# The DRAM round trips of the transposed attention units, issued from GpSimd's queue

## The chip, the cores and the metric

One core of one Trainium2 chip runs the whole layer. The metric is the device time of the kernel in microseconds; runs are compared by their median.

## What is computed

One decoder layer over 512 tokens of width 2048, all in fp32. The input is normalised, one wide projection feeds three head groups, and their gated outputs go through one output projection, with a residual add and a final normalisation:

```python
h = rmsnorm(x, norm_g)
proj = h @ w_in
...
o_cmp, o_slc = nsa_compressed_and_selected(q_a, k_cmp, v_cmp, ...)
o_win = banded_attention(q_a, ..., slopes_a, NSA_WINDOW, None)
o_a = gate[..., 0:1] * o_cmp + gate[..., 1:2] * o_slc + gate[..., 2:3] * o_win
y_a = o_a.reshape(bsz, T, A_WIDTH) * jax.nn.silu(a_z)
...
h_b = mlstm_chunkwise(...)
y_b = h_b.reshape(bsz, T, B_WIDTH) * jax.nn.silu(b_z)
...
o_c = banded_attention(..., alibi_slopes(C_HEADS), SWA_WINDOW, sinks)
y_c = o_c.reshape(bsz, T, C_WIDTH) * jax.nn.silu(c_z)
mix = jnp.concatenate([y_a, y_b, y_c], axis=-1)
return x + mix @ w_out
```

Groups A and C have 8 heads of 64, group B has 4 heads of 256.

## The kernel before

TensorE works through the columns of both projections in a fixed order: sixteen groups of input columns (`groups`) and four of output columns (`outs`). Every weight is split into a high and a low part (`wh`, `wl`), and every product is three matmuls (line 1149). A group is cut into pieces of 256 rows of the weight (512 for `ck`). The loop at the end of the program takes one piece at a time: it splits the piece two ahead (ScalarE makes `wh` in lines 162 and 164, VectorE makes `wl` in lines 170 and 172), issues the matmuls of the present one, and then starts the load of the piece five ahead (`dma_piece`, line 140). There are three buffers `raw` for these loads, so a load waits until VectorE has read the piece three before it.

Everything else runs beside this loop in "lanes", Python generators that advance by one `yield` after each set of matmuls (`step`). Their instructions fall between those of the projections, and each engine and each queue takes its instructions strictly in the order in which the program wrote them. Nothing is reordered at run time.

From the group `bo0` on, the softmax lanes run: `a_scores` and `a_out` for group A, `c_scores` and `c_out` for group C, which starts at `bz0`. One step of `a_out` takes two heads and one of two branches (selected blocks or window): eight such steps, called A0 to A7 here. Group C has four, C0 to C3, two heads each. The probabilities come out with queries on partitions, and the product with V wants keys there. The transposition goes through DRAM: `flip` takes the step's tiles one after the other (six in an A step, four in a C step). For each, `flip_out` has VectorE transpose it in 32x32 blocks into `sq` (line 613) and writes `sq` to a DRAM tile `far` (line 615); two tiles later, `flip_in` reads `far` back with the blocks in their new places (line 621, tiles `ptT` for A and `cptT` for C). The read waits for the landing of its write. After the last read and a pause of a few yields the matmuls of the step are placed in TensorE's order: line 952 (`oT`) for A, line 1035 (`coT`) for C. TensorE waits at that place if the last tile has not landed. Group B's hidden states take the same way, with four writes per pair in `hb_post` and the four reads in `ev_bz` (`hbT`), long after.

SP issues all weight loads, all writes and reads of the flips, and at the end the output. In this stretch GpSimd's queue (POOL) holds only five loads: `fg`, the final norm's gain (line 1168), and `xr` four times, the residual input (line 1174). They wait until the input projection has done with the tiles whose room they take.

Of the kernel before, what the change touches and what calls it, by code (L numbers as in the profile page):

```python
# [27 lines left out]
T, D, P = 512, 2048, 128  # L28
# [32 lines left out]
def hymba_layer(ctx, tc, x, norm_g, w_in, w_out, pe_k, w1_k, w2_k, pe_v, w1_v, w2_v, conv_w, conv_b,  # L61
                i_bias, f_bias, mnorm_g, sinks, final_g, consts, out):
    nc = tc.nc
    PE, ACT, DVE, POOL, SP = nc.tensor, nc.scalar, nc.vector, nc.gpsimd, nc.sync
# [9 lines left out]
    def U(name, dt=F32):  # L74
        return ar.tile([P, 516], dt, tag="u", name=name)
# [3 lines left out]
    def WK(name):  # L79
        return ps.tile([P, 512], F32, tag="wk", bufs=4, name=name)  # L80
# [223 lines left out]
    p = WK("gT")  # L304
# [303 lines left out]
    def flip_out(src, tag, bufs):  # L608


        n = src.shape[1]
        sq, far = U("sq"), dr.tile([P * 512], F32, name="far", tag=tag, bufs=bufs)
        DVE.transpose(sq[:, :n].rearrange("p (j b t) -> p b j t", j=4, t=32),  # L613
                      src.rearrange("p (b k j) -> p b j k", j=4, k=32))
        SP.dma_start(far[:P * n].rearrange("(p f) -> p f", p=P), sq[:, :n])
        return far, n

    def flip_in(far, name):

        dst, (src, n) = U(name), far  # L620
        SP.dma_start(dst[:, :n].rearrange("p (q f) -> p q f", q=4),
                     src[:P * n].rearrange("(q p f) -> p q f", q=4, p=P))
        return dst[:, :n].rearrange("p (q b t) -> p b q t", q=4, t=32)

    def hb_post(pair, ssq):
        yield from pause(3)
        for t in range(4):
            hb, th = B["hb", pair, t], U("bsq")
            for q in range(2):
                ACT.activation(th[:, q * 256:(q + 1) * 256], hb[:, q * 256:(q + 1) * 256], AF.Square,  # L630
                               accum_out=ssq[:, 2 * t + q:2 * t + q + 1])
            yield
        r = S("br", 8, 2)
        rsqrt(r, ssq, 256, "b")
        DVE.tensor_scalar(r, r, 0.5, None, op0=OP.mult)
        yield
        for t in range(4):
            hb = B["hb", pair, t]
            for q in range(2):
                s = slice(q * 256, (q + 1) * 256)  # L640
                DVE.tensor_scalar(hb[:, s], hb[:, s], r[:, 2 * t + q:2 * t + q + 1], None, op0=OP.mult)
            yield

        B["hbT", pair] = []
        for t in range(4):
            B["hbT", pair].append(flip_out(B.pop(("hb", pair, t))[:, :512], "hbT", 8))
            yield
# [3 lines left out]
    def ev_bz(pair):  # L651
        def ev(c, acc):
            z = U("zf")
            scaled(z[:, :512], acc)
            if c == 0:
                B["hbT", pair] = [flip_in(x, "hbT") for x in B["hbT", pair]]
            start(bz_post(pair, c, z))
        return ev
# [204 lines left out]
    def flip(parts, name):  # L863

        far, back = [], []
        for i in range(len(parts)):
            far.append(flip_out(parts[i], "far", 8))
            parts[i] = None
            if i >= 2:
                back.append(flip_in(far[i - 2], name))  # L870
            yield
        return back + [flip_in(x, name) for x in far[-2:]]
# [284 lines left out]
    for pos, (g, i) in enumerate(pieces):  # L1157
        np_ = KT // g.kps
        nct = g.n // P if g.mode == "F" else NT
        if i == 0:  # L1160
# [10 lines left out]
            if g.mode == "O":  # L1171
                n = int(g.name[3])
# [65 lines left out]
```

## Time and profile before

| | |
|---|---|
| median of 3 runs | 1028.22 us (1027.75 to 1030.64) |
| the profiled execution: its time | 1031.22 us |
| its span, first to last instruction | 1029.5 us |
| TensorE (PE) busy | 98% |
| VectorE (DVE), ScalarE (ACT) busy | 57%, 46% |
| GpSimd (POOL) busy | 2% |
| granted TensorE clock, mean | 0.989 of full speed |

All stretches are in us from the start of the span. A row of the timeline has start, duration, engine, line, operation, output and inputs, how many instructions are merged, and in brackets the idle time of the engine before the first of them and what ended it. A row of DMA issues has output and input, queue, operation, count, size of each and the median time from issue to landing. "PEclk" is the granted TensorE clock as a share of full speed: 1.00 is 2.4 GHz, 0.50 is 1.2 GHz.

### The profile page before, as it was taken

How to read it: one execution, taken by the hardware profiler on the slowest of the kernel's cores; microseconds unless marked ns; L12 is line 12 of the kernel's file. 1: busy time of each engine (PE TensorE's matmuls, PEld its weight loads, DVE VectorE, ACT ScalarE, POOL GpSimd, SP SyncE). 2: the span in 40 equal slices, each digit the busy share in tenths (PEclk: the TensorE clock that was granted, in tenths of full speed). 3: DMA queues.
4: the chain of work that ended last, by engine and by line, in shares of the span. 5: the costliest groups of instructions: out<-in, count | busy, mean ns of one | idle time of the engine just before them, and what ended most of it. 6: DMA issues, size and time to landing. Idle time of an engine off the chain costs nothing.

```text
span 1029.5 us, 13708 instructions
## 1 busy us (share of the span) xinstructions
PE 1007.5 (98%) x4967; PEld 835.0 (81%) x4967; DVE 585.6 (57%) x1253; ACT 477.5 (46%) x991; POOL 21.5 (2%) x40
## 2 busy tenths in 40 slices
PE   9999999999999999999999999999899899999996
PEld 7988888888888888888888788878777788888885
DVE  4563266664284847435566577856676575424434
ACT  6753244443253536234467474755654542323324
POOL 2400000000000000000000000000000000000000
PEclk9999999999999999999999999999999899999998
DMA  8633323232313244232335556555564685433214
GB/s 238 173 109 100 103 65 103 62 103 82 103 61 103 62 127 100 82 111 74 103 105 175 175 172 193 148 160 163 164 200 133 241 276 173 127 100 100 85 61 164
DMA packets 121092, 133.22 MB, mean 129 GB/s; under 512 B 23557, under 2 KB 81261, under 8 KB 120897
## 3 DMA queue, kind: packets, MB, share of 16 engines
q1 hardware_dynamic: 117792, 125.66, 40.9%
q0 software_dynamic: 2240, 6.23, 1.8%
q8 instruction: 39, 0.64, 0.3%
q10 hardware_dynamic: 992, 0.46, 0.2%
q14 instruction: 29, 0.23, 0.1%
HBM read 111.88 MB, written 20.45 MB: 129 GB/s over the span
## 4 chain that ended last, share of the span: by engine, by line
PE 86%; DVE 6%; DMA 5%; issue 1%; ACT 1%; SPq 0%; ACTq 0%; DVEq 0%
PE acc L1149 72%; DMA far<-sq 3%; DVE sq L613 2%; PE oT L952 2%; PE sp L561 1%; DMA ptT<-far 1%; PE acc L316 1%; PE acc L315 1%; PE acc L314 1%; DVE wl L172 1%; PE coT L1035 1%; PE sc L902 1%; PE sc L901 1%; PE xT L285 1%; DVE pp L905 0%
## 5 line engine op out<-in xcount | busy, mean ns | idle before, releaser
L1149 PE MATMUL acc<-hTh,wh 128*128 128x512 f32 x720 | 283.6, 394 | 0.0
L1149 PE MATMUL acc<-hTh,wl 128*128 128x512 f32 x720 | 281.5, 391 | 0.0
L1149 PE MATMUL acc<-hTl,wh 128*128 128x512 f32 x720 | 281.2, 391 | 0.0
L172 DVE SCALAR_TENSOR_TENSOR wl<-raw,gcol,wh 128x512 fp32r<-128x512 f32 (+1 forms) x256 | 179.0, 718 | 125.1 <-ACT wh L164 124.7
L164 ACT ACTIVATE wh<-raw,gcol 128x512 fp32r<-128x512 f32 (+1 forms) x256 | 171.2, 695 | 150.9 <-PE acc L1149 124.2
L1149 PEld LDWEIGHTS acc<-hTh,wl 128*128 128x128 f32 x720 | 135.4, 188 | 28.8
L1149 PEld LDWEIGHTS acc<-hTh,wh 128*128 128x128 f32 x720 | 135.6, 188 | 27.7 <-issue 1.7
L1149 PEld LDWEIGHTS acc<-hTl,wh 128*128 128x128 f32 x720 | 135.7, 188 | 25.8
L1149 PE MATMUL acc<-wh,hTh 128*128 128x512 f32 x256 | 101.2, 395 | 0.0
L1149 PE MATMUL acc<-wh,hTl 128*128 128x512 f32 x256 | 100.1, 391 | 0.0
L1149 PE MATMUL acc<-wl,hTh 128*128 128x512 f32 x256 | 99.9, 390 | 0.0
L1149 PE MATMUL acc<-wh,mixh 128*128 128x512 f32 x224 | 88.6, 396 | 0.0
L1149 PE MATMUL acc<-wh,mixl 128*128 128x512 f32 x224 | 88.1, 393 | 0.0
L1149 PE MATMUL acc<-wl,mixh 128*128 128x512 f32 x224 | 88.0, 393 | 0.0
L170 DVE TENSOR_TENSOR wl<-raw,wh 128x512 fp32r<-128x512 f32 x56 | 38.4, 689 | 55.7 <-ACT wh L162 55.4
L162 ACT CAST wh<-raw 128x512 fp32r<-128x512 f32 x56 | 34.0, 617 | 76.3 <-PE acc L1149 64.0
L1149 PEld LDWEIGHTS acc<-wh,hTl 128*128 128x128 f32 x256 | 48.0, 188 | 10.5
L1149 PEld LDWEIGHTS acc<-wh,hTh 128*128 128x128 f32 x256 | 48.1, 188 | 9.4 <-issue 0.4
L1149 PEld LDWEIGHTS acc<-wl,hTh 128*128 128x128 f32 x256 | 48.1, 188 | 9.0
L907 ACT ACTIVATE pp<-pp,nmx 128x512 f32<-128x512 f32 (+3 forms) x64 | 35.8, 559 | 35.1 <-DVE nmx L905 35.0
L905 DVE CUSTOM_DVE_ANT_0 pp<-sc,dmast 128x512 f32<-128x512 f32 (+3 forms) x64 | 31.1, 485 | 35.2 <-PE sc L902 35.0
L1149 PEld LDWEIGHTS acc<-wh,mixl 128*128 128x128 f32 x224 | 42.1, 188 | 10.0
(285 smaller groups left out, 1255.0 us busy)
## 6 DMA issues: line engine op xcount, KB each, us to landing
raw<-in_w_in_dram SPq DMA_DIRECT2D x80, 512.0 KB, 3.8
raw<-in_w_in_dram SPq DMA_DIRECT2D x68, 256.0 KB, 2.9
raw<-in_w_out_dram SPq DMA_DIRECT2D x32, 512.0 KB, 3.9
far<-sq SPq DMA_DIRECT2D x48, 256.0 KB, 2.8
ptT<-far SPq DMA_DIRECT2D x32, 256.0 KB, 3.9
xr<-in_x_dram POOLq DMA_DIRECT2D x4, 1024.0 KB, 8.3
x<-in_x_dram SPq DMA_DIRECT2D x12, 256.0 KB, 5.3
raw<-in_w_in_dram SPq DMA_DIRECT2D x8, 384.0 KB, 3.2
```

The source lines that it names most:

```text
L162: ACT.copy(t["h"][:, q], raw[:, j + q])
L164: ACT.activation(t["h"][:, q], raw[:, j + q], AF.Copy, scale=gcol[:, k:k + 1])
L170: DVE.tensor_tensor(t["l"][:, q], raw[:, j + q], f(t["h"][:, q]), op=OP.subtract)
L172: DVE.scalar_tensor_tensor(t["l"][:, q], raw[:, j + q], gcol[:, k:k + 1], f(t["h"][:, q]), op0=OP.mult, op1=OP.subtract)
L285: PE.transpose(p[:, q * P:(q + 1) * P], X[t][c][:, q * P:(q + 1) * P], ident)
L314: PE.matmul(acc[:, :416], HH(k, *s), G0H[k][:, :416], start=(k == 0), stop=False)
L315: PE.matmul(acc[:, :416], HL(k, *s), G0H[k][:, :416], start=False, stop=False)
L613: DVE.transpose(sq[:, :n].rearrange("p (j b t) -> p b j t", j=4, t=32), src.rearrange("p (b k j) -> p b j k", j=4, k=32))
L905: DVE.tensor_tensor_reduce(b, sp[:, :nk], dmast[:, 512 - nk:], scale=-(2.0 ** -(h + 1)), scalar=3.0e38, op0=OP.add, op1=OP.min, accum_out= ...
L907: later(lambda b=b, h=h, j=j, st=st: ACT.activation(b, b, AF.Exp, scale=-1.0, bias=st[h][0][:, j:j + 1], accum_out=st[h][1][:, j:j + 1]))
L952: PE.matmul(ob[64 * q:64 * q + 64, j * P:(j + 1) * P], VG[i][:, vo + 64 * g:vo + 64 * g + 64], tt[h][j, i], start=False, stop=(br == 2 and ...
L1149: PE.matmul(accs[c][:, :n], a, b, start=(k == 0 and q == 0), stop=(k == KT - 1 and q == 2))
```

## The change

Two words. The write to `far` and the read from it, which SP issued, are issued by GpSimd:

```diff
         DVE.transpose(sq[:, :n].rearrange("p (j b t) -> p b j t", j=4, t=32),
                       src.rearrange("p (b k j) -> p b j k", j=4, k=32))
-        SP.dma_start(far[:P * n].rearrange("(p f) -> p f", p=P), sq[:, :n])
+        POOL.dma_start(far[:P * n].rearrange("(p f) -> p f", p=P), sq[:, :n])
         return far, n

     def flip_in(far, name):

         dst, (src, n) = U(name), far
-        SP.dma_start(dst[:, :n].rearrange("p (q f) -> p q f", q=4),
+        POOL.dma_start(dst[:, :n].rearrange("p (q f) -> p q f", q=4),
                      src[:P * n].rearrange("(q p f) -> p q f", q=4, p=P))
```

It covers 72 writes and 72 reads (48 `ptT`, 16 `cptT`, 8 `hbT`). The orders of PE, DVE and ACT are the same in both kernels.

SP's queue at step A1 before. `raw` is a weight load, `far<-sq` a write, `ptT<-far` a read:

```order
L140 DMA raw<-in_w_in_dram 128x2x512
L615 DMA far<-sq 128x512
L615 DMA far<-sq 128x256
L621 DMA ptT<-far 128x4x128
L615 DMA far<-sq 128x512
L621 DMA ptT<-far 128x4x128
L615 DMA far<-sq 128x512
L621 DMA ptT<-far 128x4x64
L140 DMA raw<-in_w_in_dram 128x2x512
L615 DMA far<-sq 128x256
L621 DMA ptT<-far 128x4x128 x2
```

SP's queue in the same part of the program now, from the loads of the compression weights (`w_3554`) to the first outputs:

```order
L756 DMA w_3554<-in_cmp_w_v_dram 128x8x64
L140 DMA raw<-in_w_in_dram 128x2x512 x36
L140 DMA raw<-in_w_in_dram 128x4x128 x4
L140 DMA raw<-in_w_in_dram 128x2x512 x24
L140 DMA raw<-in_w_out_dram 128x2x512 x32
L1099 DMA out_dram<-y 128x512 x3
```

The writes and reads have gone, and the weight loads follow one another. The writes and reads keep their order among themselves on POOL.

POOL's queue at the start of the output projection, what it held before and holds now. `fg` and the first `xr` stand ahead of step C3's flips:

```order
+L621 DMA hbT<-far 128x4x128 x4
 L1168 DMA fg<-in_final_norm_g_dram 128x2048
-L1174 DMA xr<-in_x_dram 128x4x512 x4
+L1174 DMA xr<-in_x_dram 128x4x512
+L615 DMA far<-sq 128x384
+L615 DMA far<-sq 128x512
+L615 DMA far<-sq 128x384
+L621 DMA cptT<-far 128x4x96
+L615 DMA far<-sq 128x512
+L621 DMA cptT<-far 128x4x128
```

Before, `fg` was the first DMA on POOL after the parameters of the beginning. Now the flips of A0 to A7 and of C0 to C2 and both sets of `hbT` reads stand ahead of it, and three of the four `xr` come after C3's flips.

## Rows read from the trace of the kernel before

**Rows 1.** Busy time, share of the span and instructions of each engine (page, part 1)

```profile
PE 1007.5 (98%) x4967; PEld 835.0 (81%) x4967; DVE 585.6 (57%) x1253; ACT 477.5 (46%) x991; POOL 21.5 (2%) x40
```

**Rows 2.** PE's waits over the span: us in total, times, longest us

```profile
PE oT L952 <- DMA ptT<-far: 8.7, 5, 3.8
PE coT L1035 <- DMA cptT<-far: 2.7, 2, 1.6
```

**Rows 3.** Timeline of PE where it waited, at steps A1, A4, A6, A7, C1

```profile
579.55 0.44 PE L952 MATMUL oT<-ptT,vg 128*64 128x128 f32 x4 [1.68 <-DMA ptT<-far]
...
677.25 2.65 PE L952 MATMUL oT<-ptT,vg 128*64 128x128 f32 x38 [0.36 <-DMA ptT<-far]
...
740.41 0.98 PE L952 MATMUL oT<-ptT,vg 128*64 128x128 f32 x8 [2.59 <-DMA ptT<-far]
...
774.07 1.34 PE L952 MATMUL oT<-ptT,vg 128*64 128x128 f32 x16 [3.82 <-DMA ptT<-far]
...
807.92 0.40 PE L1035 MATMUL coT<-cptT,vg 128*64 128x128 f32 x2 [1.13 <-DMA cptT<-far]
809.90 1.33 PE L1035 MATMUL coT<-cptT,vg 128*64 128x128 f32 x10 [1.58 <-DMA cptT<-far]
```

**Rows 4.** Timeline of PE at steps A0, A2, A5 and C3, without a wait

```profile
548.67 2.75 PE L952 MATMUL oT<-ptT,vg 128*64 128x128 f32 x40
...
612.82 2.35 PE L952 MATMUL oT<-ptT,vg 128*64 128x128 f32 x40
...
705.91 2.40 PE L952 MATMUL oT<-ptT,vg 128*64 128x128 f32 x40
...
865.38 1.75 PE L1035 MATMUL coT<-cptT,vg 128*64 128x128 f32 x28
```

**Rows 5.** Last reads of A2, A5, C3: DMA issues at 607.5, 703.1, 860.8

```profile
ptT<-far SPq DMA_DIRECT2D x1, 128.0 KB, 2.9
...
ptT<-far SPq DMA_DIRECT2D x1, 128.0 KB, 2.2
...
cptT<-far SPq DMA_DIRECT2D x1, 256.0 KB, 2.9
```

**Rows 6.** Busy time by stretch: stretch, us, each engine (count), PEclk, DMA, GB/s

```profile
580.40:583.80 3.40, 3.40 (x34) 3.36 (x31) 0.00 (x0) 0.00 (x0) 0.00 (x0) 0.50 0.76 279
...
809.10:815.90 6.80, 6.00 (x32) 4.87 (x33) 0.00 (x0) 1.33 (x2) 0.00 (x0) 0.50 0.81 272
```

**Rows 7.** Chain that ended last: start, us, what; two sets of 34 matmuls

```profile
580.21 3.85 PE oT L952 x34
...
677.72 2.18 PE oT L952 x34
```

**Rows 8.** Writes and reads of the flips on SP: duration min/median/max, ns

```profile
L615 SPq DMA_DIRECT2D far<-sq x72: 319/333/1021, 532.3 to 855.6; - x72
L621 SPq DMA_DIRECT2D ptT<-far x48: 359/376/1082, 536.8 to 770.9; - x48
```

**Rows 9.** Timeline of POOL, the loads of the last 250 us

```profile
795.98 0.56 POOL L1168 DMA_DIRECT2D fg<-in_final_norm_g_dram  x1 [756.82 <-PE acc L1149]
...
838.59 1.49 POOL L1174 DMA_DIRECT2D xr<-in_x_dram  x2 [41.28 <-PE acc L1149]
```

**Rows 10.** DMA issues from 23.1 to 23.6, one after the other

```profile
raw<-in_w_in_dram SPq DMA_DIRECT2D x1, 152.0 KB, 2.9
raw<-in_w_in_dram SPq DMA_DIRECT2D x1, 128.0 KB, 2.1
raw<-in_w_in_dram POOLq DMA_DIRECT2D x1, 8.0 KB, 3.2
```

**Rows 11.** Landing of all 72 writes, us (line 615)

```profile
DMA to landing us min/median/max: 1.7/2.7/7.2
```

**Rows 12.** DMA issues from 797.8 to 802: a write of step C1

```profile
far<-sq SPq DMA_DIRECT2D x1, 192.0 KB, 7.2
```

**Rows 13.** Readers of `xr`: duration, first and last start us

```profile
L1075 DVE TENSOR_TENSOR y<-acc,xr x16: 682/690/692, 882.6 to 1020.2; 128x512 f32<-128x512 f32 x16
```

## The prediction

> **What bounds the kernel now.** I read the engine shares first: TensorE (PE) is busy 98% of the span [rows 1], so only what leaves PE idle, or slows its clock, can move the time. Next PE's waits: after the start it waits for nothing but the last reads of the flips, 8.7 us at A steps and 2.7 us at C steps, 11.4 in all [rows 2]. It never waits for a weight, so sparing the weight loads their wait behind the flips is worth nothing by itself. The timeline says which steps: A1 (1.7), A4 (0.4), A6 (2.6), A7 (3.8) and C1 (1.1 and 1.6) [rows 3]. The rest of the 8.7 is a second pause of 0.2 in A1.
>
> Of the steps without a wait, A0 has no slack: its 40 matmuls take 2.75 us where A2's take 2.35 [rows 4], so the last tile lands while they run. A2's last read is issued at 607.5 and lands 2.9 later, at 610.4 [rows 5]; PE uses it at 612.8, a slack of 2.4. Two more are as roomy (A3 3.0, C2 2.5, the same pair of rows). A5 lands at 705.3 and is used at 705.9, slack 0.6; C3 lands at 863.7 and is used at 865.4, slack 1.7 [rows 4, 5].
>
> A stall has a second price. After the stalls of A1, A6, A7 and C1 the granted clock stands at 0.50 (1.2 GHz): 3.4 us after A1, 6.8 after C1 [rows 6], and 3.4 after each of the other two. What 3.4 us of it cost is read from two sets of 34 equal matmuls, 3.85 us there and 2.18 at full clock [rows 7]: 1.7 us. So the flips now cost 11.4 us of idle time and about 8.5 (1.7 x 3 + 3.4) of slow clock, 20 in all. The change acts on these 20 us and on the steps that have no slack.
>
> **The change part by part.**
>
> *SP loses 144 issues.* Weight loads stand alone on SP and start when their buffer is free. PE does not wait for them, so I count nothing. Nor does the weight loads' waiting much delay the flips today: a load waits for VectorE to finish a split that stands ahead of the next transpose in VectorE's own order, so a write behind it loses only the load's issue, about 0.4 us.
>
> *POOL gains 144 issues.* On SP a write takes 0.33 us to issue and a read 0.38 [rows 8]. On POOL `fg`, with one row per partition like a write, takes 0.56, and two `xr`, with four rows per partition like a read, take 1.49, 0.75 each [rows 9]. At the end of a step one write and one read may stand ahead of the last write, 0.6 us longer than on SP; a weight load that often stood there has gone, 0.4 to 0.6. I count these against each other.
>
> *Each landing gets later.* The trace has no write or read of `far` on POOL. The nearest rows are three loads issued within half a microsecond: on SP 128 KB lands after 2.1 us and 152 KB after 2.9, on POOL 8 KB after 3.2 although it has the least to move [rows 10]. POOL's price is so between 0.3 and 1.1 us per DMA, less whatever the separate queue gives back. I take 0.6, near the middle. A step's tail is a last write, its landing, a last read, its landing: two landings, **1.2 us per step**, 0.6 and 2.2 at the ends. The Trainium skill, page "DMA: Bandwidth & Descriptors", section "Latency and other measured facts", gives about 0.6 us to the first byte for SP's path and about 1 us for GpSimd's; by it the estimate would be 0.8 per step and the estimate of the sum 2.4 us smaller, 3.3. The trace's pair reaches from less to nearly three times its 0.4 per landing.
>
> Where it falls: A0, A1, A4 and A6 have no slack, 4.8. A5 pays beyond its slack, 0.6. A2, A3, C2 and C3 are covered by their slack of 1.7 to 3. A7 shares its stretch with C0: ten writes and ten reads in one queue need 10 x 0.56 + 10 x 0.75 = 13.1 us of issue on POOL against 7.1 on SP [rows 8, 9], so I take 2.0 there. Together 7.4 us.
>
> *`fg` and the first `xr` move behind other flips.* Today they go out at 796.0 [rows 9], 2 MB in the middle of C1's flips, and a write of C1 needs 7.2 us to land [rows 12] against a median of 2.7 [rows 11]. In the new order they stand behind C2's flips and the second `hbT` reads, some 40 us later. The first reader of `xr` is at 882.6 [rows 13], so they still land in time. C1 is relieved by at most its 2.7 us of idle time and 3.4 of slow clock, 6.1. It also pays the 1.2 and has its own weight loads beside it, so I take half: 1.7 idle and 1.7 clock, **3.4 us gained**.
>
> *Clock.* With 1.2 us more A0 and A4 wait about 1.6 us each, about the smallest wait after which the trace shows 0.50 (1.7, A1); 0.4 at A4 had none after it [rows 3, 6]. I count one new stretch at the low level, 1.7.
>
> *Sum:* 7.4 - 3.4 + 1.7 = **5.7 us slower**. The profiled execution took 1031.2 (span 1029.5) and would take 1036.9 (1035.2); it lies 3.0 above the median of the runs, 1028.2, so the median becomes 1033.9.
>
> *Ends.* With 1.1 per landing, a step pays 2.2: A0, A1, A4, A6 8.8, A5 1.6, C3 0.5, A7 4, C1 gains nothing, three new stretches of slow clock 5.1: 20 slower, 1048. With 0.3 a step pays 0.6: 2.4 at the four, 0 at A5, 1 at A7, no new slow stretch, and C1 is relieved in full: 3.4 - 6.1, 2.7 faster, 1025.5.
>
> **The rivals.**
>
> *Faster: the flips' data no longer stands behind weight data.* On SP a write that follows a weight load lands after it: the median landing is 2.7 us, the shortest 1.7 [rows 11]. If the separate queue gives back this 1.0 at each of the two landings and POOL's price is at its lower end (0.3), a tail is 1.4 us shorter. A1 gains 1.4, A4 0.4, A6 1.4, A7 1.4, C1 2.7, 7.3 in all, and with the clock after C1 (3.4) nearly 11: 1017 to 1021, say 1019. It decides from the point where a landing on POOL beside weights is no later than one on SP behind them. For it: most landings today are well above the shortest. Against it: flips share the same DMA engines with weights whichever queue issues them, and weight loads which today wait behind a flip would now run beside it.
>
> *Nothing measurable:* the price per step is about 0.8, at the four 3.2, A5 0.2, A7 1.6, together 5.0, and C1's relief of 5 cancels it: 1028. The Trainium skill's page "DMA: Bandwidth & Descriptors", section "Issuing engines are not separate DMA queues", speaks for it: the engine that issues changes only the time of issue. The landings in rows 10 don't show equality.
>
> *Much slower: VectorE holds up GpSimd's issues.* If a POOL DMA must wait until a running VectorE instruction ends, each of the tail's two landings can lose up to a mean VectorE instruction, 585.6 us over 1253, 0.47 us [rows 1]: 0.9 per step, over A0, A1, A4 to A7 and C1 6.3 more, plus two slow stretches, 3.4: 1044. Against it: POOL's issues at 796 and 838 are no longer than 0.56 and 0.75 each [rows 9], with VectorE 57% busy over the span [rows 1]. The Trainium skill's page "SBUF — State Buffer", section "SBUF: two separate sides", states such a lock for some two-port VectorE instructions; no run here shows it.
>
> **How the numbers follow.** Forecast (2 to 16 slower) 0.50, much slower 0.06, nothing measurable 0.20, faster 0.24. About 0.3%, 3.1 us, is what a measurement of this kernel can tell from no change: faster means below 1025.1, slower above 1031.3. The forecast's lower edge lies inside "same", the rival "same" spreads a little to both sides; I give faster 0.25, same 0.20, slower 0.55. The likeliest case's own range is 1030 to 1044. The range over all cases, with half of "faster" in it, is 1019 to 1044.
>
> **What would show it.** Right: in the new profile A0, A1, A4, A5, A6 and A7 each wait 1 to 2 us more for `ptT`; writes and reads on POOL land 0.3 to 1.1 us later than on SP in comparable stretches; C1's wait shrinks and `fg` goes out after 830. Wrong: PE's waits for flips fall in sum below 11.4, or the medians of landing fall although POOL issues them (rival one); VectorE or ScalarE gets later by itself; or POOL's issues grow far beyond 0.75 us (rival three). A wait of PE for weights or for `xr` would be outside all of this.

## The result, and the profile after

The change costs 1.6%: 1044.41 us median (1042.63 to 1048.67) against 1027.99 for the kernel before on the same chip, a ratio of 1.016 with a 95% interval of 1.0123 to 1.0197. Slower was forecast, but by 5.7 us and not by 16.4, and the time lies just outside the range that ended at 1044.

The profiled execution took 1048.67 us, its span is 1046.9. That is 17.4 us more than the span of before, and the rows below say where they are. First the busy times and PE's waits, which answer to [rows 1, 2] (a row of waits: us in total, times, longest us):

```profile
PE 1009.7 (96%) x4967; PEld 836.2 (80%) x4967; DVE 585.9 (56%) x1253; ACT 477.1 (46%) x991; POOL 114.7 (11%) x184
...
PE oT L952 <- DMA ptT<-far: 25.5, 8, 8.3
PE coT L1035 <- DMA cptT<-far: 0.9, 2, 0.6
```

PE waits 16.8 us more at A steps and 1.8 less at C steps, and it is busy 2.2 us longer with the same 4967 instructions, which is the slower clock: together 17.2 of the 17.4. VectorE and ScalarE do what they did. The timeline of PE at A0, A1, A4, A5, A6 (two rows) and A7, against [rows 3, 4]:

```profile
549.80 2.63 PE L952 MATMUL oT<-ptT,vg 128*64 128x128 f32 x38 [0.70 <-DMA ptT<-far]
...
584.52 3.80 PE L952 MATMUL oT<-ptT,vg 128*64 128x128 f32 x34 [5.41 <-DMA ptT<-far]
...
684.42 3.90 PE L952 MATMUL oT<-ptT,vg 128*64 128x128 f32 x34 [2.93 <-DMA ptT<-far]
...
717.54 1.64 PE L952 MATMUL oT<-ptT,vg 128*64 128x128 f32 x26 [1.22 <-DMA ptT<-far]
...
753.98 0.69 PE L952 MATMUL oT<-ptT,vg 128*64 128x128 f32 x4 [4.78 <-DMA ptT<-far]
756.71 2.62 PE L952 MATMUL oT<-ptT,vg 128*64 128x128 f32 x22 [2.04 <-DMA ptT<-far]
...
795.41 3.89 PE L952 MATMUL oT<-ptT,vg 128*64 128x128 f32 x34 [8.28 <-DMA ptT<-far]
```

The steps that wait more are those that had no slack, and A5, which had 0.6: by 0.7 us (A0), 3.7 (A1, with a pause of 0.16 that isn't shown), 2.6 (A4), 1.2 (A5), 4.2 (A6) and 4.5 (A7), and not by the 0.6 to 2 of the sum. The other A steps still don't wait. The clock, against [rows 6] (stretch, us, each engine's busy time and count, PEclk, DMA share, GB/s):

```profile
581.30:588.10 6.80, 3.58 (x34) 3.57 (x36) 0.00 (x0) 0.00 (x0) 0.75 (x1) 0.50 0.31 114
683.70:690.50 6.80, 6.08 (x42) 5.33 (x43) 0.00 (x0) 0.36 (x1) 0.00 (x0) 0.50 0.26 79
751.90:762.10 10.20, 6.08 (x41) 5.16 (x42) 2.46 (x7) 4.61 (x11) 0.75 (x1) 0.50 0.43 119
789.50:799.70 10.20, 4.29 (x38) 3.99 (x38) 0.00 (x0) 0.04 (x1) 5.04 (x7) 0.50 0.81 260
```

In this part of the span PE has 34 us at 1.2 GHz where it had 17. Before, it was busy in 16 of the 17; now it is busy in only 20 of the 34, since the low level often begins inside the wait. After C1 there is none any more.

The writes on POOL, against [rows 8, 11] (duration min/median/max in ns, first and last start; then us from issue to landing):

```profile
L615 POOL DMA_DIRECT2D far<-sq x72: 539/540/568, 532.6 to 874.8; - x72
...
DMA to landing us min/median/max: 1.9/3.2/7.7
```

The shortest landing is 0.2 to 0.3 us later than on SP, the median 0.5. No write takes longer than 0.568 us to issue, with VectorE busy 56% of the span. The reads:

```profile
L621 POOL DMA_DIRECT2D ptT<-far x48: 747/759/769, 537.3 to 790.8; - x48
```

What the averages hide is seen in one stretch, the flips of A7 and C0, from A7's second write to the landing of its last read. The same view as above with PEclk, DMA share and GB/s at the end, first before, then after:

```profile
756.70:774.40 17.70, 13.88 (x67) 10.99 (x65) 12.29 (x21) 9.09 (x19) 0.00 (x0) 1.00 0.94 278
```

```profile
773.90:795.90 22.00, 13.72 (x64) 10.87 (x64) 11.99 (x20) 8.76 (x19) 15.27 (x23) 0.85 0.96 311
```

The DMA engines are 94 to 96% busy in it: the flips are here not a matter of latencies but of what is put through. Before, 17.7 us at 278 GB/s are 4.9 MB. After, 22.0 at 311 are 6.8 MB, here by queue (q0 is POOL's, q1 is SP's; packets, MB, share of the 16 engines' time):

```profile
q0 software_dynamic: 1489, 4.76, 68.4%
q1 hardware_dynamic: 1071, 2.06, 27.3%
```

SP moves nothing but weights there, 2.06 MB. The flips of the stretch are 4.19 MB by their shapes, so the weights before were about 0.7 MB. Of the 1.9 MB more, 1.4 are thus weights; the other 0.56 belong to the `hbT` reads, which now follow A7's last read on POOL directly. The timeline of SP's queue shows how they came in; before, from the first read of A7:

```profile
758.46 0.40 SPq L621 DMA_DIRECT2D ptT<-far  x1
...
759.57 1.22 SPq L140 DMA_DIRECT2D raw<-in_w_in_dram  x1
...
770.14 1.14 SPq L621 DMA_DIRECT2D ptT<-far  x2
771.33 1.02 SPq L140 DMA_DIRECT2D raw<-in_w_in_dram  x2
```

After, SP's whole queue in that stretch:

```profile
772.65 15.99 SPq L140 DMA_DIRECT2D raw<-in_w_in_dram  x4
```

Before, one load of 512 KB goes out among the flips; the next two stand in the queue behind reads that wait for landings, and go out at 771.3, after the last read. After, no flip holds SP: four loads go out between 772.7 and 788.6, three of them in the stretch shown.

### The profile page after: what moved, and what is told of

Same layout as the page of the kernel before. It is cut to its first block, busy times and chain, and to the rows that moved or that the text cites. A ratio compares the mean times of both kernels' runs of the same rounds, so it can differ in the third digit from the quotient of the medians.

```text
span 1046.9 us, 13742 instructions
## 1 busy us (share of the span) xinstructions
PE 1009.7 (96%) x4967; PEld 836.2 (80%) x4967; DVE 585.9 (56%) x1253; ACT 477.1 (46%) x991; POOL 114.7 (11%) x184
## 4 chain that ended last, share of the span: by engine, by line
issue 52%; PE 32%; DMA 8%; DVE 3%; POOL 2%; ACT 1%; SPq 0%; ACTq 0%; POOLq 0%; DVEq 0%
PE acc L1149 28%; DMA far<-sq 3%; PE oT L952 2%; DMA ptT<-far 2%; DVE sq L613 1%; DMA raw<-in_w_in_dram 1%; ACT pp L919 1%; DMA bias<-in_mlstm_i_bias_dram 1%; DMA x<-in_x_dram 1%; PE sc L902 1%; DVE wl L172 1%; PE sc L901 1%; POOL far L615 0%; POOL ptT L621 0%; PE coT L1035 0%
## 5 line engine op out<-in xcount | busy, mean ns | idle before, releaser
L615 POOL DMA_DIRECT2D far<-sq x72 | 39.3, 546 | 704.3 <-DVE sq L613 699.7
L1149 PEld LDWEIGHTS acc<-wh,hTl 128*128 128x128 f32 x256 | 48.0, 188 | 10.4
L952 PE MATMUL oT<-ptT,vg 128*64 128x128 f32 x320 | 30.2, 344 | 25.5 <-DMA ptT<-far 25.5
## 6 DMA issues: line engine op xcount, KB each, us to landing
xr<-in_x_dram POOLq DMA_DIRECT2D x4, 1024.0 KB, 11.1
```

The costliest lines, as they stand in the source:

```text
L615: POOL.dma_start(far[:P * n].rearrange("(p f) -> p f", p=P), sq[:, :n])
L952: PE.matmul(ob[64 * q:64 * q + 64, j * P:(j + 1) * P], VG[i][:, vo + 64 * g:vo + 64 * g + 64], tt[h][j, i], start=False, stop=(br == 2 and ...
L1149: PE.matmul(accs[c][:, :n], a, b, start=(k == 0 and q == 0), stop=(k == KT - 1 and q == 2))
```

## The experiments

Theory W: the loss comes from the weight loads. In one queue with the flips they stood behind reads and writes that were waiting; alone on SP they run into the bursts of flips. Theory P: it is GpSimd's own price, longer issues and later landings. From e5 on the expectations call the first theory R, in the form that weights on a queue of their own share the DMA engines with the flips. All ratios are to the kernel before on the same chip.

Two quantities are worked out from the issues and landings in each trace. The tail of an A step runs from the end of its last `sq` on VectorE to the landing of its last read, as a mean over A0 to A7 in four parts. "Loads" counts the weight loads issued from 8 us ahead of the issue of a step's last write to that of its last read, summed over the eight steps. Both come from one profiled execution of each kernel.

| kernel | last sq to write's issue | write's landing | to the read's issue | read's landing | tail, us | loads |
|---|---|---|---|---|---|---|
| before | 0.86 | 4.12 | 0.06 | 3.30 | 8.3 | 11 |
| after | 1.24 | 5.35 | 0.70 | 3.78 | 11.1 | 18 |
| e1, writes on POOL | 0.30 | 4.30 | 0.09 | 3.60 | 8.3 | 8 |
| e2, reads on POOL | 0.12 | 4.50 | 0.86 | 3.85 | 9.3 | 22 |
| e3, SP waits for each write | 1.29 | 4.67 | 0.70 | 4.85 | 11.5 | 14 |
| e4, weights on POOL, flips on SP | 0.81 | 5.26 | 0.05 | 3.76 | 9.9 | 18 |
| e5, all on POOL | 1.97 | 4.54 | 0.47 | 3.47 | 10.4 | 10 |
| e6, after with half the weights | 1.08 | 4.55 | 0.72 | 3.29 | 9.6 | 17 |
| e6b, before with half the weights | 0.78 | 3.74 | 0.07 | 3.22 | 7.8 | 12 |
| e7, writes ahead of reads | 0.30 | 2.66 | 2.04 | 5.58 | 10.6 | 17 |
| e8, SP waits for the last read | 1.09 | 4.07 | 0.73 | 2.98 | 8.9 | 6 |

**Half of the change at a time.** e1 moves line 615 alone:

```diff
-        SP.dma_start(far[:P * n].rearrange("(p f) -> p f", p=P), sq[:, :n])
+        POOL.dma_start(far[:P * n].rearrange("(p f) -> p f", p=P), sq[:, :n])
```

> Only the writes to far go to POOL; the reads stay on SP, where each read waits for its write's landing and so holds back the weight loads behind it, as in the kernel before. Theory W (the changed kernel is slow because weight loads that SP's order held behind the flips now run beside them): close to before, 1027 to 1032. Theory P (every flip DMA on POOL is later by a price of POOL's own): half of the loss, about 1036, with PE's waits for ptT near 17 us.

e2 moves line 621 alone:

```diff
-        SP.dma_start(dst[:, :n].rearrange("p (q f) -> p q f", q=4),
+        POOL.dma_start(dst[:, :n].rearrange("p (q f) -> p q f", q=4),
```

> Only the reads go to POOL; the writes stay on SP. A write waits only for VectorE, so nothing on SP waits for a landing and the weight loads are free. Theory W: most of the loss, 1039 to 1046. Theory P: half of it, about 1036.

e1: 1028.46 us, ratio 0.9988 (0.9968 to 1.0008). e2: 1035.22, 1.005 (1.0025 to 1.0076). e1 came out where W had it, e2 below W's range and where P had it. Nothing and half a per cent, and both together 1.6%: the parts don't add up, so a fixed price per DMA on POOL is unlikely to be the whole. PE's waits in e1, then in e2:

```profile
PE oT L952 <- DMA ptT<-far: 6.8, 5, 3.1
PE coT L1035 <- DMA cptT<-far: 6.3, 2, 5.5
```

```profile
PE oT L952 <- DMA ptT<-far: 13.0, 5, 7.3
PE coT L1035 <- DMA cptT<-far: 2.3, 2, 1.2
```

In e1 the A steps are better off than before (6.8 against 8.7): the reads on SP still hold the weights, and the last write no longer stands behind a read. What it lost is 5.5 us at C3, where two `xr` are now issued beside the flips. The DMA issues of e1 from 850 to 862 (KB each, median us to landing):

```profile
xr<-in_x_dram POOLq DMA_DIRECT2D x2, 1024.0 KB, 7.7
raw<-in_w_out_dram SPq DMA_DIRECT2D x3, 512.0 KB, 8.5
cptT<-far SPq DMA_DIRECT2D x2, 256.0 KB, 7.5
```

**Holding the weights at each read.** e3 is the changed kernel with 72 small loads on SP, each waiting for a write's landing as SP did before:

```diff
         dst, (src, n) = U(name), far
+        SP.dma_start(S("hold", 8, 8)[0:1, :], src[0:8].rearrange("(o f) -> o f", o=1))
         POOL.dma_start(dst[:, :n].rearrange("p (q f) -> p q f", q=4),
```

> The changed kernel, and at the place of each read SP also loads 32 bytes from the same far tile into a small tile. SP so waits for the same landings as before, and the weight loads behind it are held again; reads and writes stay on POOL. Theory W: the loss goes, 1028 to 1034, A7's wait falls from 8.3 us to 4 to 5. Theory P: as the changed kernel or slower, 1044 to 1047.

1057.94 us, 1.0264 (1.0233 to 1.0294): worse than the change, and outside what either theory gave. The last write lands earlier than after the change (4.67 against 5.35), the last read later (4.85 against 3.78). At A7, SP is held until 791.0 and then lets two weight loads go at once, just as POOL issues the last read; SP, then POOL:

```profile
778.33 12.66 SPq L621 DMA_DIRECT2D hold<-far  x9
791.08 0.91 SPq L140 DMA_DIRECT2D raw<-in_w_in_dram  x2
```

```profile
791.31 0.75 POOL L622 DMA_DIRECT2D ptT<-far  x1 [0.41 <-ACT zth L663]
```

Before, such a load stood behind the read in one queue; here it travels beside it. The 72 more DMAs have a price too, which this run doesn't part from that. I gave up the form of W that a hold at the write's landing is enough, and for a while W with it, too early, as e8 shows.

**The other way round.** e4 leaves the flips on SP and moves the weights:

```diff
-            SP.dma_start(raw[:, :, o:o + b - a], src.rearrange("(k p) c -> p k c", p=P))
+            POOL.dma_start(raw[:, :, o:o + b - a], src.rearrange("(k p) c -> p k c", p=P))
```

> The queues are exchanged: weight loads on POOL, the flips alone on SP. The weight loads run freely beside the flips, and the flips pay none of POOL's price. Theory W: slower than before, 1036 to 1044. Theory P: no loss, 1022 to 1029; fg and the first xr also leave C1's flips here, since they stand behind weight loads on POOL.

1048.4 us, 1.0163 (1.0126 to 1.02), above W's range too. No flip is issued on POOL here, and it costs as much as the change. PE's waits:

```profile
PE oT L952 <- DMA ptT<-far: 18.5, 6, 8.3
PE coT L1035 <- DMA cptT<-far: 4.4, 3, 3.6
PE acc L1149 <- DVE wl L170: 2.7, 3, 1.7
```

So parting the two queues is enough for most of a loss of this size, without POOL's price on any flip: PE waits 9.8 us more at the A steps and 1.7 more at the C steps. It also waits 2.7 for late `wl`. Those three waits lie between 860 and 874, after `fg` and the first `xr` have gone out in the weights' queue (845.6); their cause was not tested, and e5, with weights on POOL too, has none.

**One queue again, on POOL.** e5 has e4's edit on top of the change, so that POOL holds the order that SP held.

> Weight loads go to POOL as well, so weights and flips stand in one queue again, in the order of the kernel before, and every one of them pays POOL's price. Theory R (two queues share the DMA engines, so that weight data issued after a flip takes part of its bandwidth, while in one queue it comes behind): 1029 to 1037, A7's wait back to about 5 us. Theory P (POOL's own price per DMA makes the loss): 1044 or more.

1042.23 us, 1.015 (1.0127 to 1.0174), near the change. Loads among the flips are back at 10 and the landings near those of before (4.54 and 3.47). What is new is the issue: a weight load takes 0.72 us on POOL, and the last write goes out 1.97 us after its `sq`. PE's wait, the rows of L140 and a piece of POOL's timeline at A7:

```profile
PE oT L952 <- DMA ptT<-far: 19.2, 10, 5.4
...
L140 POOL DMA_DIRECT2D raw<-in_w_in_dram x164: 704/722/762, 37.1 to 820.9; - x164
...
770.57 0.54 POOL L615 DMA_DIRECT2D far<-sq  x1
771.10 0.72 POOL L140 DMA_DIRECT2D raw<-in_w_in_dram  x1
```

One queue keeps the order, but here every issue in it takes longer. The time lies between the two expectations, and the run does not tell the theories apart, since it takes one cause away and enlarges the other.

**Half of the weights.** e6 is the changed kernel and e6b the kernel before, both with the second half of each piece not loaded in six groups and the four outputs (the first half is used twice, so half of those weights is left out). The line that does it; the splits in lines 162 to 172 then read the first half for both:

```diff
         for a, b in g.segs:
+            if g.name in HALF:
+                b = a + 256
             src = g.w[i * kps * P:(i + 1) * kps * P, a:b]
```

> The changed kernel, but the weight loads of the groups bo0 to bz1 (not ck) and of the output projection fetch 256 of the 512 columns, and the splits read these twice, so the weights' DMA traffic in the stretch of the flips halves and the work of all engines stays. Half of those weights is left out of the result. Theory R: PE's waits for ptT fall from 25 us to 12 to 17, the time to 1032 to 1038. Theory P: waits and time as in the changed kernel, 1042 to 1045.

> The kernel before with the same halved weight loads (half of those weights is left out of the result), as the control. Theory R: a little faster, 1020 to 1026, since weight data that stands ahead of a flip in the one queue is halved too; the distance to the run with POOL shrinks from 16 us to about 10. Theory P: the distance stays at 16.

With half of the weights the changed kernel takes 1033.03 us, 1.0052 (1.0032 to 1.0071), the kernel before 1027.09, 0.9988 (0.9975 to 1.0002). The kernel before gains next to nothing, where R had 1020 to 1026. The distance between the two shrinks from 16.4 to 5.9 us. The waits of the first and of the second:

```profile
PE oT L967 <- DMA ptT<-far: 15.0, 9, 4.5
```

```profile
PE oT L967 <- DMA ptT<-far: 6.6, 5, 4.5
PE coT L1050 <- DMA cptT<-far: 3.5, 2, 2.0
```

POOL's issues are the same in both changed kernels, the weights' bytes aren't. Two thirds of the loss go when half of these bytes go, more than R had it, which left some 10 us.

**The order within POOL.** e7 takes away what makes the last write stand behind waiting reads on POOL:

```diff
-            far.append(flip_out(parts[i], "far", 8))
+            far.append(flip_out(parts[i], "far", 12))
             parts[i] = None
-            if i >= 2:
-                back.append(flip_in(far[i - 2], name))
             yield
-        return back + [flip_in(x, name) for x in far[-2:]]
+        return back + [flip_in(x, name) for x in far]
```

> The changed kernel, with one edit: each step issues all its writes before its first read (with 12 buffers of far instead of 8), so that on GpSimd's queue no write stands behind a read that waits for a landing. Nothing is left out. If the one queue is what costs (the last write of a step is issued 1.24 us after its sq is ready, against 0.3 where writes and reads had a queue each): that falls to about 0.3, each A step's tail is 0.9 us shorter, six steps without slack gain some 5 to 7 us with their slow clock, and the time is 1036 to 1040. If the landings beside weight loads are what costs: reads bunch up behind the last write, the last read is issued no earlier, and the time stays at 1042 to 1047.

1041.22 us, 1.0133 (1.0102 to 1.0165), between the two and not to be told from the change itself. The last write goes out after 0.30 us and lands in 2.66, but the reads bunch up: the last is issued 2.04 us after its write's landing and lands in 5.58. The sum of the tail hardly moves (10.6 against 11.1). The data that has to go through is the same. PE's waits at the A steps are shorter all the same, 18.8 us in the profiled execution, and the tail's mean doesn't say why.

**Holding the weights over the whole tail.** e8 is the changed kernel with 12 small copies; SP waits for the landing of each step's last read:

```diff
-        return back + [flip_in(x, name) for x in far[-2:]]
+        back += [flip_in(x, name) for x in far[-2:]]
+        SP.dma_start(S("hold", 8, 8)[0:1, :], back[-1][0:1, 0, 0, 0:8])
+        return back
```

> The changed kernel, and one small DMA more per step (12 in all): SP copies 32 bytes of the step's last ptT (or cptT) tile into a small tile. It waits for the landing of the step's last read, so on SP no weight load is issued between the place of that copy in the program and the landing: the last write and the last read of each step travel with no new weights beside them. Nothing is left out. If weight loads beside the flips are a large part of the loss: the last write lands in about 4.5 us instead of 5.35 and the last read in about 3.3 instead of 3.8 (what they took with half of the weights), the tail falls from 11.1 to about 9.7 us, and the time to 1034 to 1039, unless PE comes to wait for weights (then a wait for wl shows). If GpSimd's own price is nearly all: tail 10.7 to 11.2 and 1042 to 1047.

1029.53 us against 1030.32, a ratio of 0.9998 (0.9973 to 1.0024): the whole loss is gone, more than the 1034 to 1039 expected of the weights, with every flip still on POOL. SP's queue in the stretch of A7 and C0, from 755 to 776, and the stretch itself as above:

```profile
755.01 0.37 SPq L140 DMA_DIRECT2D raw<-in_w_in_dram  x1
772.77 0.67 SPq L873 DMA_DIRECT2D hold<-cptT  x1
774.45 0.63 SPq L873 DMA_DIRECT2D hold<-ptT  x1
775.18 0.90 SPq L140 DMA_DIRECT2D raw<-in_w_in_dram  x2
```

```profile
756.20:774.50 18.30, 13.76 (x64) 10.87 (x64) 12.04 (x20) 8.82 (x19) 15.13 (x23) 0.92 0.85 269
```

```profile
PE oT L954 <- DMA ptT<-far: 10.2, 6, 4.5
```

One weight load goes out at the start of the burst (755.0) and none more until the last reads have landed. The stretch takes 18.3 us and not 22.0, and moves 4.9 MB as before the change. The last write lands in 4.07 and the last read in 2.98, no later than on SP before. PE waits for no weight: there is no row for `wl` or `acc`. So the held loads come early enough.

**The relief of C1 alone.** b1 is the kernel before with `fg` and the first `xr` issued late, from SP (the second and third `xr` are issued from SP too):

```diff
-                POOL.dma_start(FG, final_g.rearrange("(o c n) -> o c n", o=1, c=4).to_broadcast([P, 4, 512]))
...
-                POOL.dma_start(XR[n], x[0, :, n * 512:(n + 1) * 512].rearrange("(t p) c -> p t c", p=P))
+                if n:
+                    (POOL if n == 3 else SP).dma_start(
+                        XR[n], x[0, :, n * 512:(n + 1) * 512].rearrange("(t p) c -> p t c", p=P))
+        if g is outs[0] and i == 5:
+            SP.dma_start(FG, final_g.rearrange("(o c n) -> o c n", o=1, c=4).to_broadcast([P, 4, 512]))
+            SP.dma_start(XR[0], x[0, :, 0:512].rearrange("(t p) c -> p t c", p=P))
```

> The kernel before, its flips and weights all on SP; only the loads of fg and the first xr are issued later, from SP's queue at piece 5 of out0, and the second and third xr from SP at the start of out1 and out2. Nothing is left out. It prices the relief of C1 by itself. If the 2 MB of fg and xr were what made C1 wait: its two waits of 1.1 and 1.6 us and the 6.8 us at half clock behind them are gone, the A steps wait the 8.7 us that they waited before, and the time falls by 4 to 6 us, to 1022 to 1025. Then the change has paid about 20 us at the A steps, of which 4 to 6 came back at C1. If C1 waits for the weights beside it: its waits stay within 1 us of 2.7 and the time is 1027 to 1029.

1024.57 us, 0.9969 (0.9943 to 0.9994), some 3 us faster, a little less than the 4 to 6 expected. Its only waits for flips are those at A steps:

```profile
PE oT L952 <- DMA ptT<-far: 8.6, 5, 3.7
```

**Better versions.** b2 joins e1 and b1's edit: writes on POOL, reads and weights on SP, `fg` and `xr` late. b4 adds e8's copy at the A steps.

> The writes alone on POOL, reads and weights on SP, and fg and the first xr are issued from SP at piece 5 of out0, the second and third xr from SP at the start of out1 and out2. If the 2 MB loads cost C1 (before) or C3 (writes on POOL) their waits: 1017 to 1023, PE's waits for cptT below 2 us. If they do not: 1027 to 1030.

> The kernel with the writes on GpSimd's queue, the reads and the weights on SP's, fg and xr late, and at each of the eight A steps one more 32-byte copy on SP that waits for the landing of the last read, so that no weight load is issued between the last read's issue and its landing. Nothing is left out. In this queue a weight load already stands behind the reads; the copy only holds the loads that would follow the last read. If a load issued behind the last read, on the same queue, still delays its landing: the A steps' waits of 5.2 us shrink to 2 to 3 and the time is 1013 to 1017. If a load behind the read on the same queue does no harm (what matters is loads in the burst ahead of the last read, and those on another queue): 1018 to 1021. Above 1022 the held weights would come too late somewhere.

b2: 1019.09 us, 0.9919 (0.9902 to 0.9936). b4: 1018.77, 0.9893 (0.9864 to 0.9921). Both beat both kernels; from one to the other there is no difference that these runs can tell. PE's waits for flips, first b2, then b4:

```profile
PE oT L952 <- DMA ptT<-far: 5.2, 4, 3.2
```

```profile
PE oT L955 <- DMA ptT<-far: 4.5, 3, 3.2
```

In b2 the loads that follow the last read stand behind it on the same queue. Holding them longer brings nothing measurable, so behind the read they do little harm; on a queue of their own they did.

## Why the prediction was right in sign and wrong in size

**What bounds the kernel: right.** PE's waits for the flips' last reads and the clock behind them carry 17.2 of the 17.4 us, at the steps that were named as having no slack and at A5, which had little.

**"SP loses 144 issues ... so I count nothing": the step that failed.** I asked only whether PE or the flips gain when weights and flips no longer wait for each other, and not what the weights do once they are free. They start as soon as a buffer is free, and that is during the bursts of flips: 18 loads among the tails and not 11, three and not one at A7, where the DMA engines are already 94% busy. The price is read from the ratios of the change and of e8 to the kernel before: 1.016 and 0.9998, 1.6% or 16 us, with the intervals nowhere near each other. The changed kernel with its loads held is at the time of before. My own text had the cause, as an argument against the rival that is faster ("weight loads which today wait behind a flip would now run beside it"), but gave it no price. It was there to be had: the stretch of A7 and C0 in the trace of before shows DMA at 0.94, and two loads of 512 KB behind the last read.

The Trainium skill, page "DMA: Bandwidth & Descriptors", section "Issuing engines are not separate DMA queues", says that DMAs issued by different engines end on the same 16 DMA engines and interleave there, and that issuing on several engines saves just the issue time. The first half agrees with the bursts: the loads on SP's queue and the flips on POOL's together keep the engines 96% busy, and the flips get through later. The second half made the rival "nothing measurable"; here the choice of the issuing engine moved 1.6%, by what else it let start.

**"POOL gains 144 issues", counted at zero: undersized.** Writes take 0.54 us and reads 0.76 on POOL, as the rows of `fg` and `xr` had it. With landings as before (e8), what remains of POOL's price in the tail is 0.23 us more before the last write and 0.67 more before the last read, 0.9 in all. The second is mostly the issue of the read ahead of it. The sum had 2.0 us for the longer issues at A7; in e8 the longest wait, 4.5, is A7's, against 3.8 before.

**"Each landing gets later", 1.2 us per step: the wrong cause.** The landings did get later in the changed kernel, by 1.23 and 0.48 us, more than the 1.2 of the sum. But in e8, where the flips are still on POOL and the loads are held, they are 0.05 and 0.32 earlier than in the kernel before. So the lateness comes with the weights and not with POOL. POOL's own price is in the issue and comes to 0.54 us of tail (8.87 against 8.33). For the time: e8 has the relief of C1, about 3 us by b1, and ends at the time of before. POOL's own price is thus about 3 us, uncertain by as much, and more if the fewer loads in e8's tails (6 against 11) gained something; I had 7.4 and 1.7 of clock.

**"`fg` and the first `xr` move": right.** They went out here:

```profile
854.47 0.55 POOL L1168 DMA_DIRECT2D fg<-in_final_norm_g_dram  x1
855.00 0.75 POOL L1174 DMA_DIRECT2D xr<-in_x_dram  x1
```

C1 waits 0.85 us instead of 2.7 and has no stretch at 1.2 GHz behind it. b1 puts the relief at about 3 us by itself; the sum had 3.4.

**Clock: undersized, with the waits.** The sum had 1.7 us for one new stretch, and as much given back at C1: nothing net. PE's busy time grew by 2.2 net. By the rows, its busy time at 1.2 GHz went from 10 to 20 us at the A steps, which costs about 5 us, and the 6.0 us after C1 went, which gives 3 back. There are 17 us more at the low level in all, but PE idles through much of them.

**The rivals.** "Much slower" gave 1044, which is the time measured, by a mechanism that isn't there: all 72 writes take between 539 and 568 ns to issue on POOL, all 48 reads of the A steps between 747 and 769, and in e8, with VectorE as busy, the landings on POOL are no later than on SP. A right number for a wrong reason is no support. "Faster" has a grain in it, though not as told. In e1, with writes and reads on two queues, the last write goes out 0.30 us after its `sq` and not 0.86, and the A steps wait 1.9 us less.

**What stays open.** The count of loads does not order all kernels: e2 has 22, the most, and loses 0.5%. Its last write goes out after 0.12 us, which gives 0.7 back, and only A7 with four loads is hit hard (7.3 us); why that write still lands in 4.50 and not in the 5.35 of the change was not settled. Nor was it tested what the larger packets on POOL (below) are worth. Nor was e5's 1.5% split between its slower issues and its landings.

## What to carry to other kernels

A queue is also a brake: before a latency-bound chain is given a queue of its own, ask what used to stand behind it, and what that will do at the moment the chain is running. If it is bulk data that nobody waits for, keep it behind the chain, in the same queue or with a small DMA that waits for the chain's end, as e8 does without PE waiting for a weight. Look at the DMA share of the very stretch in which the chain runs, not at its mean over the span.

## What the runs showed of the hardware that was not expected

- In these runs two queues gave the flips no right of way over the loads. Flips on SP with weights on POOL (e4) land as late as the other way round: last write 5.26 and 5.35 us, against 4.12 with both on SP.
- A load behind a read on the same queue does little harm to it: with and without such loads (b2 and b4) 1019.09 and 1018.77 us. With loads let go beside it on another queue (e3) the last read took 4.85 us, against 3.30 before; e3 also has 72 small DMAs more.
- With the weight loads held, flips on POOL land as early as on SP among weights (2.98 against 3.30 us for the last read). The shortest of all writes stays 0.2 to 0.3 us later: 1.9 us against 1.7 [rows 11].
- The low clock can begin inside a wait and be spent there. At A7 after the change it begins at 789.5 and the wait ends at 795.4; of 34 us at 1.2 GHz, PE is busy in 20.
- The same flips go in larger packets from POOL than from SP. The stretch of A7 and C0, with nearly the same bytes, in the kernel before and in e8:

```profile
DMA packets 6937, 4.92 MB, mean 278 GB/s; under 512 B 2368, under 2 KB 5952, under 8 KB 6935
...
DMA packets 1641, 4.93 MB, mean 269 GB/s; under 512 B 321, under 2 KB 321, under 8 KB 1640
```

  The DMA engines are busy for 94% of 17.7 us in the first and for 85% of 18.3 us in the second, 16.6 and 15.6 us. Moving a DMA to another engine's queue here changed more than its place in the order.
